# A hybrid decoder block on one core: Strassen lows in two pieces, a pause between two fetches into one stage, and a shorter list behind the output units

## The chip, the cores and the metric

The kernel runs on one core of a Trainium2 chip. The metric is the device time of one execution in microseconds (us). Before the change three runs took 2387.95, 2391.85 and 2394.31 us; the median, 2391.85, is the time before.

## The reference

For T = 256 tokens and D = 4096 channels, all in float32:

```python
h = rmsnorm(x, norm_w)
proj = einsum('bsd,de->bse', h, w_in)             # 4096 -> 20480 columns
u_p, z_p, u_c, b_c, c_c, z_c, g_logit = split(proj)
y_pool = causal_multiscale_pool(u_p, pool_w, pool_scale) * silu(z_p)
y_conv = causal_gated_shortconv(u_c, b_c, c_c, conv_w, conv_b) * silu(z_c)
br = einsum('bsnc,ncd->bsnd', stack([y_pool, y_conv]), w_branch)
merged = sum(sigmoid(g_logit + gate_b) * br, over the two branches)
x = x + einsum('bsd,de->bse', merged, w_out)
return rmsnorm(x, final_norm_w)
```

Three large products (`w_in`, `w_branch`, `w_out`) make up nearly all of the work; the mixers between them are short.

## The kernel before

**Numbers in two parts.** Every float32 operand is split into a *high* (a copy rounded to the matmul's format, by ScalarE, `act`, line 59) and a *low* (operand less high, by VectorE, `sub` through line 62). A product is three matmuls: high by high, low by high, high by low. TensorE is PE in the profile, VectorE DVE, ScalarE ACT, GpSimd POOL, SyncE SP.

**Units and steps.** A unit makes 1024 output columns (`NU`) for all tokens, in 16 steps of 256 rows of the contraction (8 in the branch units). The units run one after the other: those of `w_in` (the last two gate units are g1_3 and g1_0), then `w_branch` (b0_0, b1_0, ... b1_3), then `w_out` (o0 to o3). A step is plain (P) or a Strassen step (S), which needs seven products instead of eight on sums and differences of the four blocks of the weights; S steps use the banks `shared` beside `sums`.

**Weights.** A step's weights, four blocks of 128x512, are loaded by SP into one of five slots `raw` (some parts by POOL's queue, with accumulation). `ring` has 26 cells of 128x512 for highs and lows. For an S step ACT writes the highs of blocks 0 to 2 (one 128x1536 instruction where the cells lie side by side), DVE writes their lows (`whole`), and then DVE overwrites the slot: block 1 with block 3 less block 1 (`raw<-raw 128x512`), then blocks 0 and 2 with their differences from the new block 1 (128x1024). From these the four *formed* operands come, in two pairs, `outer` and `inner`, each a high of 128x1024 on ACT and a low of 128x1024 on DVE.

**Activations.** The left operands lie in `arena` (`last_pair` and `side` hold a few). While the last gate unit and the first branch unit run, the places of x's operands are refilled with y's (kept in DRAM as `y_d`), and later with those of the merged m (`m_d`). A `Fill` does that: a 256 KB fetch into one of three stages `sa`, `sb`, `sc` (issued on ACT's queue, line 83), after `LANDING` ticks the Strassen sums on DVE (S operands only), the high `arena<-sa` on ACT and the low `arena<-sa,arena` on DVE, which is the last reader of the stage.

**What sets the order.** Every instruction is pinned to program order on its engine. A *tick* is six matmuls. At each tick one item is popped from `queue`, the list of the work that follows a finished unit, and `pop_fill` takes one step of one `Fill` or issues one fetch. `gap(n)` is n empty items; `flush()` issues all that is left of the list at once. The list of an output unit (`epi` in `out_unit`) adds x's rows to the result `E` (POOL's accumulating transfers `E<-in_x_dram`, after those of the Strassen corners `E<-J`), loads the final norm's weights into `Y`, squares the two halves of `E` on ACT (`Y<-E`, with the sums of squares into `ossq`), multiplies `E` by the weights on DVE (`E<-E,Y`), and stores the result (`o_d`). The list of o0 is worked off while o1 runs, and so on; o3 has its own ending (`finish`), before which `flush()` and `last.before()`, the load of its final weights, are called at a fixed step.

Of the kernel before, what the change touches and what calls it, by code (L numbers as in the profile page):

```python
# [15 lines left out]
P = 128  # L16
# [3 lines left out]
NU = 1024  # L20
# [31 lines left out]
def hybrid_block(ctx: ExitStack, tc: tile.TileContext, x, xc, prm, rows_in, w_in, pool_w, w_branch, w_out, out):  # L52
# [11 lines left out]
    def mul(dst, a, b):  # L64
        return tt(dst, a, b, ALU.mult)
# [16 lines left out]
    def move(dst, src):  # L82
        return pin(nc.scalar.dma_start(dst, src))
# [140 lines left out]
    rg = Ring()  # L224

    def runs(cells):
        at = 0
        while at < len(cells):
            n = 1
            while at + n < len(cells) and cells[at + n] == cells[at] + n:  # L230
                n += 1
            yield slice(at, at + n), slice(cells[at], cells[at] + n)
            at += n

    def pieces(a, b):
        at = 0
        while at < len(a):
            n = 1
            while at + n < len(a) and a[at + n] == a[at] + n and b[at + n] == b[at] + n:
                n += 1  # L240
            yield slice(at, at + n), slice(a[at], a[at] + n), slice(b[at], b[at] + n)
            at += n

    def highs(cells, src):
# [3 lines left out]
    def lows(to, cells, src):  # L248
        for i, c, o in pieces(cells, to):
            sub(ring[:, o], src[:, i], ring[:, c].bitcast(F32))  # L250
# [7 lines left out]
    class Step:  # L258
# [28 lines left out]
        def rest(self):  # L287
            if self.kind == "P":
                def rests(to):
                    self.lows = to  # L290
                    if self in steps[:2]:
                        for i in range(4):
                            if self is steps[0] and i % 2 == 0:
                                x_low(0, 1 - i // 2)
                            lows(to[i:i + 1], self.cells[i:i + 1], self.q[:, i:i + 1])
                    elif self.halved:
                        for i in (0, 2):
                            lows(to[i:i + 2], self.cells[i:i + 2], self.q[:, i:i + 2])
                    else:
                        lows(to, self.cells, self.q)  # L300

                return [(4, None, rests)] + self.mid
            if self.kind == "S":
                def whole(to):
                    self.lows = to
                    lows(to, self.cells, self.q[:, 0:3])

                def outer(cells):
                    q = self.q
                    self.outer = cells  # L310
# [191 lines left out]
    def gap(n):  # L502
        return [None] * n
# [264 lines left out]
    def out_unit(c):  # L768
        cs = slice(c * NU, (c + 1) * NU)

        def start():
            move(Y[:, 0], final_w[None, cs].to_broadcast([P, NU]))

        def epi(u):
            def row(t):
                gather(E[:, t], xrows[:, t, cs])

            def square(t):
                act(Y[:, 1], E[:, t], AF.Square, accum_out=ossq[:, t, c:c + 1])
            return gap(6) + [lambda: row(0), None, lambda: row(1)] + gap(12) + [start] + gap(8) + [  # L780
                lambda: square(0), lambda: square(1),
                lambda: mul(E, E, Y[:, 0:1].to_broadcast([P, 2, NU]))] + gap(5) + [lambda: move(o_d[c], E)]

        text = (SIX5, NINE, NINE, OUT3)[c]
        u = Unit(f"o{c}", lambda i: w_out[c, i], seq_x(text), m_ops, epi, before=start if c == 3 else None)
        u.late = c < 3
        units.append(u)
# [16 lines left out]
    class Fill:  # L804
# [9 lines left out]
        def advance(self, force):  # L814
            o, q = self.o, self.st[:, 0:self.o.n] if self.o.kind == "S" else self.st[:, 4:8]
            if not force and (now[0] < self.due or (self.phase != 1 and now[0] < quiet[0])):
                return False
            if self.phase == 0 and o.kind == "S":
                sums_s(self.st)
                self.phase, self.due = 1, now[0] + 4  # L820
            elif self.phase < 2:
                act(o.view[:, 0], q)
                self.phase, self.due = 2, now[0] + 1
            else:
                sub(o.view[:, 1], q, o.view[:, 0].bitcast(F32))
                o.ready = True
                fills.remove(self)
            return True

    stages = [sa]  # L830
    fills = deque()
    now, quiet, hush = [0], [0], [0]
    LANDING, STORED, QUIET, HUSH = 12, 7, 5, 20

    def pop_fill(force=None):
        now[0] += 1
        for f in list(fills):
            if f.at is not None and f.free() and (now[0] >= f.at + LANDING or f.o is force):
                if f.advance(f.o is force):
                    break  # L840
        used = [f.st for f in fills if f.at is not None]
        nxt = next((f for f in fills if f.at is None), None)
        if nxt is None or not nxt.ready() or now[0] < hush[0]:
            return
        st = next((q for q in stages if not any(q is u for u in used)), None)
        if st is not None:
            nxt.fetch(st)

# [334 lines left out]
    for st in lead:  # L1183
# [1 line left out]
        run_step(last, st)  # L1185
        state["now"] += 1
        pump()
        if st is lead[len(lead) // 2]:
            flush()
            last.before()  # L1190
        if not combined and last.closed(FB):
# [83 lines left out]
```

## Time and profile before

| | |
|---|---|
| runs | 2387.95, 2391.85, 2394.31 us |
| profiled execution, its own time | 2388.57 us |
| its span (first to last instruction) | 2386.9 us |
| mean granted TensorE clock | 0.995 |
| ACT busy / DVE busy / POOL busy | 1489.8 / 2140.5 / 288.3 us |
| mean DMA rate | 263 GB/s |

How to read the rows: a row of the timeline gives start and length in us, engine, source line, operation, what is written from what is read, the number of instructions drawn together, and in brackets how long the engine had been idle before it and what released it. `ACTq` is ACT's sequencer issuing a transfer. In rows of groups stand the number, busy time, mean duration in ns, and the idle time before. The line is mostly that of a helper, so tiles tell instructions apart. The profiled execution's time is 1.7 us longer than its span.

### The profile page before, as it was taken

Reading aid. Unit: us, or ns where it says so; the run is one execution under the profiler, and the core shown is the slowest. Engines: PE = TensorE matmul, PEld = TensorE weight load, DVE = VectorE, ACT = ScalarE, POOL = GpSimd, SP = SyncE. Lnnn points to the kernel's source line nnn. Section 1 sums busy time; section 2 is a strip of 40 time slices with the busy share of each in tenths; the row PEclk is TensorE's granted clock in tenths of the full one; section 3 lists DMA queues with packets and bytes.
Section 4 is the critical chain, followed back from the end, with each engine's and each line's share of the span. In section 5 each row is a group of like instructions: output and inputs, shape, how many; then the busy total and the mean of one; then the engine's idle time right before and its main releaser. Section 6 shows DMA issues by size and latency. Waiting matters only on the chain. (4 is left out here: it accounts for less than half of the span.)

```text
span 2386.9 us, 28585 instructions
## 1 busy us (share of the span) xinstructions
PE 2349.5 (98%) x10424; PEld 1938.9 (81%) x10424; DVE 2140.5 (90%) x1986; ACT 1489.8 (62%) x1565; POOL 288.3 (12%) x342
## 2 busy tenths in 40 slices
PE   9999999999999999999999999999899999999997
PEld 7888888888888888888888888887778887878885
DVE  8799988999979979979999999987798889899997
ACT  6665655756656656656766676665656556566664
POOL 0001100111001201201111111110000000011110
PEclk9999999999999999999999999999999999999999
DMA  9789877988868768768999999999869788879996
GB/s 385 240 255 280 251 239 215 282 259 250 265 219 244 264 206 248 256 203 253 289 277 279 281 310 285 282 277 281 260 206 292 252 256 290 263 220 283 295 268 256
DMA packets 167709, 627.68 MB, mean 263 GB/s; under 512 B 17424, under 2 KB 25872, under 8 KB 135568
## 3 DMA queue, kind: packets, MB, share of 16 engines
q1 hardware_dynamic: 101792, 485.40, 56.6%
q0 software_dynamic: 48128, 98.59, 23.3%
q10 hardware_dynamic: 17648, 41.87, 4.9%
q8 instruction: 81, 1.33, 0.2%
q14 instruction: 60, 0.49, 0.1%
HBM read 579.66 MB, written 25.17 MB: 253 GB/s over the span
## 5 line engine op out<-in xcount | busy, mean ns | idle before, releaser
L59 ACT ACTIVATE ring<-raw 128x1024 fp32r<-128x1024 f32 (+3 forms) x1089 | 1226.6, 1172 | 768.9 <-DVE raw L62 530.1
L1053 PE MATMUL sums<-ring,arena 128*128 128x512 f32 x7011 | 1647.0, 390 | 20.5 <-DVE ring L62 10.1
L62 DVE TENSOR_TENSOR ring<-raw,ring 128x1024 fp32r<-128x1024 f32 (+3 forms) x1116 | 1452.0, 1338 | 135.2 <-ACT ring L59 66.9
L1053 PEld LDWEIGHTS sums<-ring,arena 128*128 128x128 f32 x7011 | 1314.5, 188 | 301.0 <-DVE ring L62 15.7
L1053 PE MATMUL shared<-ring,arena 128*128 128x512 f32 x2241 | 541.9, 389 | 0.8 <-DVE ring L62 0.8
L1053 PEld LDWEIGHTS shared<-ring,arena 128*128 128x128 f32 x2241 | 420.7, 188 | 89.1 <-DVE ring L62 1.5
L62 DVE TENSOR_TENSOR raw<-raw 128x512 f32<-128x512 f32 (+1 forms) x444 | 425.6, 959 | 16.6 <-DMA raw<-in_w_out_dram 2.4
L89 POOL DMA_DIRECT2D raw<-in_w_in_dram x168 | 145.5, 866 | 1361.3 <-DMA raw<-in_w_in_dram 688.3
L62 DVE TENSOR_TENSOR J<-J 128x512 f32<-128x512 f32 (+1 forms) x90 | 78.2, 869 | 16.2 <-ACT J L59 14.0
L1053 PE MATMUL sums<-ring,last_pair 128*128 128x512 f32 x306 | 78.1, 396 | 2.3 <-DVE ring L62 2.3
L59 ACT ACTIVATE J<-shared 128x512 f32<-128x512 f32 x128 | 69.7, 599 | 5.5 <-PE shared L483 2.0
L1053 PEld LDWEIGHTS sums<-ring,last_pair 128*128 128x128 f32 x306 | 58.5, 191 | 15.1 <-DVE ring L62 2.7
L59 ACT ACTIVATE E<-sums 128x512 f32<-128x512 f32 x76 | 42.1, 597 | 27.5 <-PE sums L1053 26.5
L89 POOL DMA_DIRECT2D raw<-in_w_out_dram x31 | 27.4, 883 | 262.4 <-DMA raw<-in_w_out_dram 99.7
L89 POOL DMA_DIRECT2D raw<-in_w_branch_dram x23 | 20.0, 869 | 314.2 <-DVE ring L62 127.5
L1053 PE MATMUL shared<-ring,last_pair 128*128 128x512 f32 x216 | 51.9, 389 | 0.0
L1053 PE MATMUL shared<-ring,side 128*128 128x512 f32 x207 | 50.7, 389 | 0.0
L1053 PEld LDWEIGHTS shared<-ring,last_pair 128*128 128x128 f32 x216 | 40.5, 188 | 8.4
L1053 PEld LDWEIGHTS shared<-ring,side 128*128 128x128 f32 x207 | 38.9, 188 | 8.1
L89 POOL DMA_DIRECT2D E<-J x28 | 38.9, 1469 | 17.3 <-ACT ring L59 17.3
L62 DVE TENSOR_TENSOR E<-E,Y 128x2048 f32<-128x2048 f32 x9 | 20.6, 2290 | 10.0 <-ACT Y L59 10.0
L59 ACT ACTIVATE E<-E 128x1024 f32<-128x1024 f32 x16 | 16.7, 1049 | 11.4 <-DMA E<-in_x_dram 11.4
(121 smaller groups left out, 596.7 us busy)
## 6 DMA issues: line engine op xcount, KB each, us to landing
raw<-in_w_in_dram SPq DMA_DIRECT2D x150, 1024.0 KB, 7.3
raw<-in_w_in_dram SPq DMA_DIRECT2D x168, 768.0 KB, 6.6
raw<-in_w_in_dram SPq DMA_DIRECT2D x176, 256.0 KB, 5.1
raw<-in_w_in_dram POOLq DMA_DIRECT2D x168, 256.0 KB, 6.7
raw<-in_w_branch_dram SPq DMA_DIRECT2D x41, 1024.0 KB, 7.0
raw<-in_w_out_dram SPq DMA_DIRECT2D x33, 1024.0 KB, 7.0
raw<-in_w_out_dram SPq DMA_DIRECT2D x31, 768.0 KB, 7.4
raw<-in_w_branch_dram SPq DMA_DIRECT2D x23, 768.0 KB, 6.1
```

The lines of the kernel that those rows point to most:

```text
L59: return pin(nc.scalar.activation(dst, src, func, **kw))
L62: return pin(nc.vector.tensor_tensor(out=dst, in0=a, in1=b, op=op))
L89: return pin(nc.gpsimd.dma_start(dst, src, accum_op=ALU.add))
L1053: pin(nc.tensor.matmul(ps, lhs, rhs, start=n == 0, stop=n == u.total[b] - 1))
```

## The change

1. `whole` makes the low of block 1 first, as one 128x512, and then those of blocks 0 and 2 as one instruction with a stride (128x2x512). For that `pieces` and `runs` may step by two. Where the cells wrap around the ring's end there are three of 128x512.
2. When a `Fill` has finished, its stage rests for five ticks (`REST`) before the next fetch may go into it. `LANDING` is 8 ticks instead of 12.
3. The list of an output unit is 28 items long instead of 39: three empty items instead of six before the first row, three instead of twelve before the load of `Y`, nine instead of eight before the first square, one between the squares, four instead of five before the store. In o3 the `flush()` and the load of `Y` come at the tenth of 13 steps instead of the seventh; by then the shorter list is empty.

```diff
     def pieces(a, b):
         at = 0
         while at < len(a):
-            n = 1
-            while at + n < len(a) and a[at + n] == a[at] + n and b[at + n] == b[at] + n:
+            n, d = 1, 1
+            if at + 1 < len(a) and a[at + 1] - a[at] == b[at + 1] - b[at] in (1, 2):
+                n, d = 2, a[at + 1] - a[at]
+            while n > 1 and at + n < len(a) and a[at + n] - a[at + n - 1] == b[at + n] - b[at + n - 1] == d:
                 n += 1
...
                 def whole(to):
                     self.lows = to
-                    lows(to, self.cells, self.q[:, 0:3])
+                    c, q = self.cells, self.q
+                    lows(to[1:2], c[1:2], q[:, 1:2])
+                    lows([to[0], to[2]], [c[0], c[2]], q[:, 0:3:2])
...
-            return gap(6) + [lambda: row(0), None, lambda: row(1)] + gap(12) + [start] + gap(8) + [
-                lambda: square(0), lambda: square(1),
-                lambda: mul(E, E, Y[:, 0:1].to_broadcast([P, 2, NU]))] + gap(5) + [lambda: move(o_d[c], E)]
+            return gap(3) + [lambda: row(0), None, lambda: row(1)] + gap(3) + [start] + gap(9) + [
+                lambda: square(0), None, lambda: square(1),
+                lambda: mul(E, E, Y[:, 0:1].to_broadcast([P, 2, NU]))] + gap(4) + [lambda: move(o_d[c], E)]
...
                 fills.remove(self)
+                rested[id(self.st)] = now[0] + REST
...
-    LANDING, STORED, QUIET, HUSH = 12, 7, 5, 20
+    LANDING, STORED, QUIET, HUSH, REST = 8, 7, 5, 20, 5
+    rested = {}
...
-        st = next((q for q in stages if not any(q is u for u in used)), None)
+        st = next((q for q in stages if not any(q is u for u in used) and now[0] >= rested.get(id(q), 0)), None)
...
-        if st is lead[len(lead) // 2]:
+        if st is lead[-4]:
             flush()
             last.before()
```

**First place: ACT in b0_0, where the y operands are fetched (about 1721 to 1733 us in the profile).** Before, the two fetches into `sb` and `sc` stand between the copies of the banks `shared` into `J`, ahead of the copies `E<-sums`:

```order
L59 ACTIVATE arena<-sb 128x1024
L59 ACTIVATE J<-shared_85 128x512
L83 DMA sb<-y_d 128x512
L59 ACTIVATE J<-shared_86 128x512
L59 ACTIVATE J<-shared_88 128x512
L83 DMA sc<-y_d 128x512
L59 ACTIVATE ring<-raw 128x1024 x2
L59 ACTIVATE J<-shared_87 128x512
L59 ACTIVATE ring<-raw 128x1536
L59 ACTIVATE E<-sums_82 128x512
L59 ACTIVATE E<-sums_84 128x512
```

The same place on ACT after the change:

```order
L59 ACTIVATE arena<-sb 128x1024
L59 ACTIVATE J<-shared_85 128x512
L59 ACTIVATE J<-shared_86 128x512
L59 ACTIVATE J<-shared_88 128x512
L59 ACTIVATE ring<-raw 128x1024 x2
L59 ACTIVATE J<-shared_87 128x512
L59 ACTIVATE ring<-raw 128x1536
L59 ACTIVATE E<-sums_82 128x512
L59 ACTIVATE E<-sums_84 128x512
L83 DMA sb<-y_d 128x512
L59 ACTIVATE E<-sums_81 128x512
L59 ACTIVATE E<-sums_83 128x512
```

The fetch into `sb` has moved behind two of the copies `E<-sums`; that into `sc` comes later still.

**Second place: ACT in o1, where the list of o0 is worked off (about 2157 to 2179 us).** Before, from the load of `Y` to the squares:

```order
L83 DMA Y<-in_rows_dram 128x1024
L59 ACTIVATE ring<-raw 128x1024 x4
L59 ACTIVATE ring<-raw 128x1536
L59 ACTIVATE ring<-raw 128x1024
L59 ACTIVATE side<-sa 128x512
L59 ACTIVATE ring<-raw 128x1024 x3
L59 ACTIVATE Y,ossq<-E 128x1024 x2
```

After:

```order
L83 DMA Y<-in_rows_dram 128x1024
L59 ACTIVATE ring<-raw 128x1024 x2
L59 ACTIVATE ring<-raw 128x1536
L83 DMA sa<-m_d 128x512
L59 ACTIVATE ring<-raw 128x1024 x2
L59 ACTIVATE ring<-raw 128x1536
L59 ACTIVATE Y,ossq<-E 128x1024 x2
L59 ACTIVATE ring<-raw 128x1024 x4
L59 ACTIVATE ring<-raw 128x1536
```

The squares have moved ahead of nine ring highs: the four of 128x1024 that before began at 2162.84 us, the next 128x1536, and four more. On DVE, at the same place, the product stood behind the lows of the following step:

```order
L62 TENSOR_TENSOR ring<-raw,ring 128x1024 x4
L62 TENSOR_TENSOR sa<-sa 128x128 x4
L62 TENSOR_TENSOR ring<-raw,ring 128x1536
L62 TENSOR_TENSOR raw<-raw 128x512
L62 TENSOR_TENSOR raw<-raw 128x2x512
L62 TENSOR_TENSOR ring<-raw,ring 128x1024 x2
L62 TENSOR_TENSOR side<-sa,side 128x512
L62 TENSOR_TENSOR E<-E,Y 128x2048
```

After the change it stands between the first of those four lows and the second:

```order
L62 TENSOR_TENSOR ring<-raw,ring 128x512
L62 TENSOR_TENSOR ring<-raw,ring 128x2x512
L62 TENSOR_TENSOR raw<-raw 128x512
L62 TENSOR_TENSOR raw<-raw 128x2x512
L62 TENSOR_TENSOR ring<-raw,ring 128x1024
L62 TENSOR_TENSOR E<-E,Y 128x2048
L62 TENSOR_TENSOR ring<-raw,ring 128x1024 x3
```

These rows also show the split low: two instructions, 128x512 and 128x2x512, where one of 128x1536 stood, ahead of the two that overwrite the slot.

**Third place: POOL in o3, where the list of o2 is worked off (about 2295 to 2335 us).** Before, a weight load stands between the two transfers of x's rows:

```order
L89 DMA E<-J 128x2x512
L89 DMA raw<-in_w_out_dram 128x512
L89 DMA E<-J 128x2x512
L89 DMA E<-in_x_dram 128x1024
L89 DMA raw<-in_w_out_dram 128x512
L89 DMA E<-in_x_dram 128x1024
L89 DMA raw<-in_w_out_dram 128x512 x2
```

After, both rows go ahead of it:

```order
L89 DMA E<-J 128x2x512
L89 DMA raw<-in_w_out_dram 128x512
L89 DMA E<-J 128x2x512
L89 DMA E<-in_x_dram 128x1024 x2
L89 DMA raw<-in_w_out_dram 128x512 x3
```

In the other output units POOL's order is unchanged.

More of the change, by code (lines that the diff above doesn't have):

```diff
@@ L226, in runs @@
     def runs(cells):
-        at = 0
-        while at < len(cells):
-            n = 1
[L230 to L233, printed above, removed]
+        for i, c, _ in pieces(cells, cells):
+            yield i, c
     def pieces(a, b):
@@ L237, in pieces @@
         while at < len(a):
-            n = 1
-            while at + n < len(a) and a[at + n] == a[at] + n and b[at + n] == b[at] + n:
+            n, d = 1, 1
+            if at + 1 < len(a) and a[at + 1] - a[at] == b[at + 1] - b[at] in (1, 2):
+                n, d = 2, a[at + 1] - a[at]
+            while n > 1 and at + n < len(a) and a[at + n] - a[at + n - 1] == b[at + n] - b[at + n - 1] == d:
                 n += 1
-            yield slice(at, at + n), slice(a[at], a[at] + n), slice(b[at], b[at] + n)
+            yield slice(at, at + n), slice(a[at], a[at] + d * (n - 1) + 1, d), slice(b[at], b[at] + d * (n - 1) + 1, d)
             at += n
```

## The prediction

> **What bounds the kernel now.** I read the page first, then the waits of TensorE, the busy time by stage, and, at each place where TensorE stands still, the timelines of the engines that feed it.
>
> ```profile
> PE 2349.5 (98%) x10424; PEld 1938.9 (81%) x10424; DVE 2140.5 (90%) x1986; ACT 1489.8 (62%) x1565; POOL 288.3 (12%) x342
> ...
> PE sums L1053 <- DVE ring L62: 12.3, 12, 2.3
> ```
>
> TensorE (PE) is busy for 2349.5 of 2386.9 us, and the change takes no matmul away. What it can win is the rest, 37.4 us; of its waits (us in all, times, longest) that for DVE's lows is the largest. By stage:
>
> ```profile
> 1640.00:1770.00 130.00, 118.72 (x501) 95.56 (x500) 108.23 (x116) 76.39 (x84) 7.76 (x9) 0.96 0.74 234
> ...
> 1945.00:2126.00 181.00, 174.54 (x769) 141.83 (x768) 160.22 (x158) 108.40 (x119) 14.27 (x16) 0.99 0.82 257
> 2126.00:2300.00 174.00, 174.00 (x770) 144.01 (x768) 161.28 (x143) 108.50 (x115) 26.23 (x28) 1.00 0.91 272
> ...
> 2300.00:2386.00 86.00, 71.51 (x313) 58.22 (x311) 68.83 (x74) 42.70 (x49) 6.53 (x7) 0.94 0.81 275
> ```
>
> The second number is the stretch, the third PE's busy time. While the y operands are fetched (1640 to 1770, units g1_0 to b1_0) PE is idle for 11.3 us, while the m operands are fetched (1945 to 2126) for 6.5 us, and in o1 and o2 (2126 to 2300) for none. These are the three terms of the sum: the first two can only fall, the third can only rise.
>
> **The later fetch, y operands.**
>
> ```profile
> 1668.45 2.14 PE L1053 MATMUL sums<-ring,last_pair 128*128 128x512 f32 x7 [2.27 <-DVE ring L62]
> ...
> 1731.39 8.90 PE L1053 MATMUL sums<-ring,arena 128*128 128x512 f32 x31 [6.09 <-ACT E L59]
> ...
> 1760.87 4.37 PE L1053 MATMUL sums<-ring,arena 128*128 128x512 f32 x18 [1.54 <-DVE ring L62]
> ```
>
> ```profile
> 1667.29 0.33 ACTq L83 DMA_DIRECT2D sc<-y_d  x1
> 1667.72 1.49 ACT L59 ACTIVATE ring<-raw 128x1536 fp32r<-128x1536 f32 x1 [1.18 <-DVE arena L62]
> ...
> 1726.99 2.00 ACT L59 ACTIVATE ring<-raw 128x1024 fp32r<-128x1024 f32 x2 [1.72 <-DVE arena L62]
> ...
> 1730.75 2.05 ACT L59 ACTIVATE E<-sums 128x512 f32<-128x512 f32 x4
> ```
>
> A fetch is issued by ACT, and it overwrites the stage that DVE's low (`arena`) still reads. ACT itself waits for that low (1.18 and 1.72 us in these rows), and behind the issue in ACT's order stand the highs for the next weights and, at 1730.75, the copies of the banks (`E<-sums`) for which PE waits 6.09 us. With five ticks of rest (a tick is six matmuls of 2349.5 / 10424 = 0.225 us, so 6.8 us) the low is done before ACT comes to the issue, and the issue costs its 0.33 us. The first order piece shows that both issues leave the place ahead of `E<-sums`. Stall by stall: 2.27 goes; 6.09 shrinks to about 2.3, because ACT comes to `E<-sums` earlier by 1.72 and by what the issue before it held (1.18 of the same kind), and 0.6 of issues, about 3.8 with what the earlier highs give; 1.54 falls to 0.6, since DVE runs less late. The rest of the 11.3, 1.4 in small stalls of the same kind, goes too: 2.27 + 3.8 + 0.9 + 1.4 = 8.4 us of idle time. The ends: 11.3 if every stall goes, 6 if 2.27 and 3.8 alone are won. I stand nearer the upper end, because every one of these waits lies behind a fetch that moves.
>
> Can the later fetch be late for its reader? It is given less time to land, 8 ticks instead of 12, or 10.8 us.
>
> ```profile
> DMA to landing us min/median/max: 3.2/6.6/9.2
> ```
>
> This is the landing of `sa` in the stretch: the longest is 9.2 us, 1.6 under 10.8. The fetch is 5 ticks later, its use allowed 4 earlier; the high comes out one tick later at worst. I cost it at nothing; the cover is that 1.6 us.
>
> **The later fetch, m operands.**
>
> ```profile
> 2013.78 6.89 PE L1053 MATMUL sums<-ring,arena 128*128 128x512 f32 x29 [1.66 <-DVE ring L62]
> ...
> 2025.34 25.24 PE L1053 MATMUL sums<-ring,arena 128*128 128x512 f32 x110 [1.05 <-DVE ring L62]
> ...
> 2119.43 0.73 PE L1053 MATMUL sums<-ring,arena 128*128 128x512 f32 x2 [2.33 <-ACT arena L59]
> ```
>
> ```profile
> 2118.44 0.93 ACT L59 ACTIVATE arena<-sa 128x896 fp32r<-128x896 f32 x1
> ```
>
> The last operand's high stands at 2118.44 behind four ring highs, and PE waits for it. With the shorter landing it stands behind two of the four, some 2 us earlier: 1.9 won. 0.9 of 1.66 and 1.0 of 1.05 follow as for y, and 0.9 of the 1.4 in small ones. Together 4.7 us, between 2.5 (half of the three rows) and 6.5 (the whole stage).
>
> **The shorter list of a w_out unit.** The list of o0 runs in o1, that of o1 in o2, that of o2 in o3. Its squares (ACT) need x's rows, added into `E` by POOL's accumulating transfers.
>
> ```profile
> 2154.96 0.86 POOL L89 DMA_DIRECT2D E<-in_x_dram  x1 [7.21 <-DMA E<-J]
> ...
> 2228.87 1.24 POOL L89 DMA_DIRECT2D E<-in_x_dram  x1
> 2239.66 0.86 POOL L89 DMA_DIRECT2D E<-in_x_dram  x1 [9.55 <-DMA E<-J]
> ...
> 2308.53 1.81 POOL L89 DMA_DIRECT2D E<-in_x_dram  x1
> ...
> 2321.16 0.86 POOL L89 DMA_DIRECT2D E<-in_x_dram  x1 [7.23 <-DMA E<-J]
> ...
> DMA to landing us min/median/max: 12.9/12.9/12.9
> ...
> DMA to landing us min/median/max: 11.6/14.6/17.7
> ...
> DMA to landing us min/median/max: 10.6/13.0/15.5
> ```
>
> POOL stands idle for `E<-J` before each second row, so three ticks fewer in the list bring it no earlier. The last three rows are landings: of the second row in o1, and of both rows in o2 and o3 (least the second, most the first). The second rows land at 2154.96 + 12.9 = 2167.8, 2239.66 + 11.6 = 2251.3 and 2321.16 + 10.6 = 2331.8. Now look at what surrounds the new places of the squares in o1 and o2:
>
> ```profile
> 2162.84 4.09 ACT L59 ACTIVATE ring<-raw 128x1024 fp32r<-128x1024 f32 x4 [2.69 <-PE sums L1053]
> ...
> 2163.94 4.66 DVE L62 TENSOR_TENSOR ring<-raw,ring 128x1024 fp32r<-128x1024 f32 x4
> ...
> 2168.70 2.88 PE L1053 MATMUL shared<-ring,arena 128*128 128x512 f32 x12
> ...
> 2249.68 2.88 PE L1053 MATMUL shared<-ring,arena 128*128 128x512 f32 x12
> ...
> L62 DVE TENSOR_TENSOR E<-E,Y 128x2048 f32<-128x2048 f32 x9 | 20.6, 2290 | 10.0 <-ACT Y L59 10.0
> ```
>
> In o1 both squares now stand ahead of these four highs. The second waits for 2167.8 and ends at 2169.1 (1.06 and the readout); the first high follows, its low ends near 2171.4. PE reads that low in the fifth matmul of the twelve that begin at 2168.70, at 2169.6: +1.9 us. Then the product `E<-E,Y` (2.29 us) stands between the first low and the second, which ends at 2174.8 where PE wants it at 2171.0 + 1.9: another +2.0, in all 3.9. In o2 the first square stands ahead of the third ring high and the second after it, so the second waits until 2251.3; by the same steps from the twelve that begin at 2249.68 the third low is 2.9 late, and the product pushes the next one to 4.8 in all. So the cover is gone in both: +8.7 us. Its ends: 0, if the highs and lows that already lie in the ring carry PE over; 8.7 plus each microsecond by which a row lands later.
>
> In o3 it is the other way.
>
> ```profile
> 2331.83 1.06 ACT L59 ACTIVATE Y<-E 128x1024 f32<-128x1024 f32 x1 [6.21 <-DMA E<-in_x_dram]
> ...
> 2337.03 1.43 PE L1053 MATMUL sums<-ring,arena 128*128 128x512 f32 x5 [1.96 <-DVE ring L62]
> ...
> 2340.16 2.12 PE L1053 MATMUL shared<-ring,arena 128*128 128x512 f32 x8 [0.76 <-DVE ring L62]
> ```
>
> Here the early `flush()` already puts the squares ahead of the row, and PE waits 1.96 and 0.76 behind them. The squares keep their place but for one ring high. But POOL now issues the second row ahead of a weight load that stood before it in the same queue (third order piece). In o2, with no load between them, the second row lands 4.7 us after the first (2251.3 less 2228.87 + 17.7); in o3 7.8 us after it (2331.8 less 2308.53 + 15.5). Taken as in o2, it lands 3 us earlier, and both waits go: −2.7; ends −2.7 and 0, if the row only takes as long as the 11.6 and 12.9 of the other units.
>
> **The split low of a Strassen step.**
>
> ```profile
> L62 DVE TENSOR_TENSOR ring<-raw,ring 128x1024 fp32r<-128x1024 f32 x834 | 989.5, 1223 | 68.6 <-PE sums L1053 39.5 <-ACT ring L59 25.9
> ...
> L62 DVE TENSOR_TENSOR ring<-raw,ring 128x1536 fp32r<-128x1536 f32 x184 | 323.0, 1755 | 40.9 <-ACT ring L59 19.6 <-PE sums L1053 7.8 <-ACT E L59 6.1
> ...
> L62 DVE TENSOR_TENSOR ring<-raw,ring 128x512 fp32r<-128x512 f32 x46 | 31.4, 687 | 4.4 <-ACT ring L59 4.1
> ...
> 2343.56 1.76 DVE ring L62
> 2345.34 0.70 DVE raw L62
> 2346.07 1.24 DVE raw L62
> ```
>
> No low with a stride stands in the trace; the strided difference of the same size, the last row, takes 1.24 us, and a plain low 1.22, so I take 1223 ns. Alone, 687 + 1223 ns replace 1755: +155 ns, 184 times, 28.5 us of DVE. But four lows of 1223 took 4.66 us above, a pitch of 1146 ns: an instruction that doesn't wait for its neighbour starts some 80 ns before that one's end. The difference `raw` after the low did wait (2345.34 less 2343.56 is 1.78, more than 1755). Afterwards it overwrites the middle block, whose low is two instructions back. So 607 + 1143 = 1750 against 1780: −30 ns a step at best, +125 if the new order helps nothing. That is −6 to +23 us of DVE, which has 246 idle; PE would see it only where it waits for a low, and takes it as 0, ends 0 and +1.9 (0.155 at each of the 12 waits). By the Trainium skill, "VectorE: DVE Perf Modes", section "The DRAIN you can't avoid", the next operation starts only when the pipe is empty and a semaphore costs nothing; by that the split would cost its 28.5 us of DVE whole. The trace's pitch of 1146 ns for lows of 1223 disagrees (the section itself excepts operations that aren't held).
>
> **The sum.** A wait that goes is worth some 0.16 us more than its row shows: a row counts the last matmul before it with its whole duration, and while the pitch is 0.23 us (twelve matmuls take 2.88 us, 110 take 25.24), twelve pitches are 2.72. For some twelve waits that go that is 1.9 us. So −8.4 − 4.7 − 2.7 − 1.9 + 8.7 + 0 = −9.0 us. The profiled run took 2388.57; it lies 3.3 under the median of 2391.85, which I take as the level that counts, so the predicted time is 2391.85 − 9.0, or 2383.
>
> **Rivals.**
> 1. The out units cost nothing, because ACT and DVE run far enough ahead in the ring: −17.7, 2374. For it: PE had no idle time there at all. Against: the lows in question end 4 to 5 us before their use (first low near 2165.2, used at 2169.6), and the squares' wait takes 6.2. 15%.
> 2. Half of the fetches' gain only, because the next stall moves up (`E<-sums` or a later arena high takes the place of the fetch): half of 14.7 (8.4 + 4.7, and 1.6 of the 1.9), so −7.3 + 8.7 − 3.0 = −1.6, 2390. For it: DVE is 90% busy, and part of the stalls are charged to `ring` lows. 25%.
> 3. Slower: the rows land later. The load of the final weights into `Y` now starts beside the second `E<-J`, and the squares stand so early that PE loses each microsecond of a later landing, three times. From 4.4 us per row on it decides (without o3's 3.0 the gains are 14.7, 7.2 more make it measurably slower: 14.7 + 7.2 − 8.7 = 13.2 over three units). At 6 us: 2391.85 − 14.7 + 8.7 + 18 = 2404. Landings above differ by 2.3 us, those of `sa` by 6. 10%.
> 4. The split doesn't spare the wait: +125 ns a step on DVE. At the waits +1.9, and as much again where it meets the out units' lateness: −9 + 4 = −5, 2387. 5%.
>
> **How the numbers follow.** A measurement here tells about 0.3%, 7.2 us, from no change: faster is below 2384.7. The forecast has 45%, with a range of its own of −14 to −4 (2378 to 2388), two thirds of it faster: 0.31, and with rival 1 0.46. Same: 0.12 of the forecast, rival 2 but 0.03, rival 4: 0.41. Slower: rival 3 and 0.03 for worse than rival 2: 0.13. The range of 8 in 10 takes in rival 1 with 3 us to spare and rival 2, and leaves out the worse half of rival 3: 2371 to 2396.
>
> **What would show it.** PE's idle time in the y stretch falls from 11.3 to about 2, in the m stretch from 6.5 to 1.5. ACT's `ring` rows after a fetch no longer name DVE `arena`. In o1 and o2 new PE waits for `ring` lows, of 2 to 3 us each, two per unit, with ACT `Y<-E` waiting for `E<-in_x_dram` before them; in o3 the wait of 6.21 is gone. Rows of DVE `raw` 128x512 start before the 128x2x512 low ends. The prediction fails if o1 and o2 stay without idle time, or if the fetch stretches keep theirs.

## The result, and the profile after

The changed kernel takes 2385.38 us (median of 16 runs, 2379.93 to 2389.32), the kernel before 2394.14 us in the same sessions (2387.95 to 2398.84). The ratio is 0.9966 with a 95% interval of 0.9957 to 0.9974: 8 us faster, where 9 were forecast. The profiled execution of the change took 2385.66 us, with a span of 2383.9 and a clock of 0.995.

The page and the waits of TensorE over the whole span of the changed kernel:

```profile
PE 2346.6 (98%) x10424; PEld 1938.5 (81%) x10424; DVE 2138.2 (90%) x2208; ACT 1488.3 (62%) x1565; POOL 287.0 (12%) x342
...
PE sums L1054 <- DVE ring L62: 11.1, 8, 3.0
PE shared L1054 <- ACT ring L59: 5.5, 2, 4.5
```

The wait for `ACT E` that was 6.6 us is no longer among the largest, and a new one stands there: 5.5 us for highs (`ring`) of ACT. By stage (the columns as before; the third from the end is TensorE's granted clock):

```profile
1640.00:1770.00 130.00, 126.54 (x555) 103.56 (x554) 118.34 (x130) 84.62 (x93) 9.49 (x11) 1.00 0.84 261
...
1945.00:2126.00 181.00, 177.70 (x798) 146.53 (x797) 167.57 (x184) 111.36 (x123) 14.66 (x16) 1.00 0.83 255
2126.00:2300.00 174.00, 165.19 (x714) 134.63 (x713) 151.10 (x151) 102.00 (x107) 24.94 (x28) 0.98 0.90 266
2300.00:2386.00 86.00, 66.78 (x287) 54.46 (x285) 61.89 (x73) 37.40 (x44) 5.83 (x7) 0.90 0.73 248
```

TensorE's idle time in the y stretch fell from 11.3 to 3.5 us, in the m stretch from 6.5 to 3.3, and where o1 and o2 run it rose from none to 8.8. What is left of the y stretch, and ACT at the place of the first order piece:

```profile
1719.36 3.03 PE L1054 MATMUL sums<-ring,arena 128*128 128x512 f32 x12 [1.09 <-ACT E L59]
...
1748.44 3.92 PE L1054 MATMUL sums<-ring,arena 128*128 128x512 f32 x16 [1.88 <-DVE ring L62]
```

```profile
1717.03 0.37 ACTq L83 DMA_DIRECT2D sb<-y_d  x1
1717.33 1.49 ACT L59 ACTIVATE ring<-raw 128x1536 fp32r<-128x1536 f32 x1
1718.71 2.06 ACT L59 ACTIVATE E<-sums 128x512 f32<-128x512 f32 x4
```

The fetch is issued while ACT works, with no bracket of idle time behind it, and `E<-sums` costs PE 1.09 us instead of 6.09. In o1 the order piece on the squares turned out as follows (POOL, then ACT, PE and DVE):

```profile
2142.54 0.86 POOL L89 DMA_DIRECT2D E<-in_x_dram  x1 [11.22 <-DMA E<-J]
...
2149.05 1.06 ACT L59 ACTIVATE Y<-E 128x1024 f32<-128x1024 f32 x1 [7.45 <-DMA E<-in_x_dram]
...
2153.36 1.06 ACT L59 ACTIVATE Y<-E 128x1024 f32<-128x1024 f32 x1 [3.17 <-DMA E<-in_x_dram]
...
2154.42 5.26 ACT L59 ACTIVATE ring<-raw 128x1024 fp32r<-128x1024 f32 x5
...
2155.51 0.79 PE L1054 MATMUL shared<-ring,arena 128*128 128x512 f32 x1 [4.46 <-ACT ring L59]
2156.77 2.93 PE L1054 MATMUL shared<-ring,arena 128*128 128x512 f32 x6 [0.47 <-DVE ring L62]
2160.10 1.14 PE L1054 MATMUL shared<-ring,arena 128*128 128x512 f32 x2 [0.41 <-DVE ring L62]
...
2155.49 1.22 DVE L62 TENSOR_TENSOR ring<-raw,ring 128x1024 fp32r<-128x1024 f32 x1 [7.75 <-ACT ring L59]
2156.63 2.29 DVE L62 TENSOR_TENSOR E<-E,Y 128x2048 f32<-128x2048 f32 x1
```

ACT stands 10.6 us for x's rows. PE waits 4.46 us for the first high behind the squares, 0.47 for that high's low, and 0.41 for the next low, which stands behind the product.

**A ledger.** Both kernels run the same 10424 matmuls in the same order, so the start of the n-th one can be compared between any two traces. Differences to the first profile of before, in us (minus is earlier); the ending is the time from the last matmul's start to the span's end:

| matmuls | what runs | forecast | change | change again | before again |
|---|---|---|---|---|---|
| to 7400 | w_in | 0 | −0.2 | 0.2 | 0.2 |
| 7400 to 7800 | y operands | −8.4 | −12.2 | −10.6 | 0.0 |
| 7800 to 8600 | branches | 0 | 0.5 | 0.1 | 0.5 |
| 8600 to 9400 | m operands | −4.7 | −6.6 | −6.6 | 0.9 |
| 9400 to 9600 | o1 | 3.9 | 8.2 | 8.7 | 0.0 |
| 9600 to 10000 | o2 | 4.8 | 4.3 | 7.7 | 0.0 |
| 10000 to the last | o3 | −2.7 | 0.6 | −1.0 | 2.5 |
| ending | | 0 | 2.4 | −0.3 | 2.9 |
| span | | | −3.0 | −1.7 | 7.0 |

(The forecast's 1.9 us for the uncounted part of the waits belongs to the y, m and o3 rows.) The last two columns are two of the experiments below.

**What the rows of the ledger are made of.** Only a part of each row is idle time of TensorE. Differences to the first profile of before, in us:

| stage | idle time: forecast | change | again | the rest of the row: change | again |
|---|---|---|---|---|---|
| y operands | −8.4 | −7.8 | −7.8 | −4.4 | −2.8 |
| m operands | −4.7 | −3.2 | −3.3 | −3.4 | −3.4 |
| o1 | 3.9 | 5.3 | 6.3 | 2.8 | 2.4 |
| o2 | 4.8 | 3.5 | 3.6 | 0.8 | 4.2 |
| o3 | −2.7 | −0.7 | −1.0 | 1.3 | 0.0 |

The rest lies in the matmuls around and behind a wait. The last one before it counts with its whole duration (the 0.16 us of the forecast), and the first one behind it is followed after 0.34 us instead of 0.23, which is 0.11 more. Behind some waits the granted clock also stood at 0.50, for 3.41 us or twice that. Each 3.41 us held some eight matmuls, 0.43 us apart, and so cost some 1.6 us. Before, this happened behind the waits of 2.27, 6.09 and 2.33 us; in the change it happened behind the 4.46 us in o1 and behind a wait of 2.06 us in o3. Four windows show it: one of before (behind 2.27), one of the change in o1, one of the change in o2, and one of its second profile in o2:

```profile
1669.95:1673.35 3.40, 3.40 (x9) 2.64 (x8) 3.33 (x4) 1.16 (x2) 0.00 (x0) 0.50 1.02 422
```

```profile
2154.20:2161.01 6.81, 4.62 (x9) 2.92 (x10) 5.52 (x4) 5.47 (x7) 0.62 (x1) 0.50 0.18 50
...
2241.00:2251.00 10.00, 6.53 (x27) 4.50 (x26) 8.46 (x8) 5.13 (x7) 0.86 (x1) 1.00 0.88 223
```

```profile
2248.00:2254.80 6.80, 6.08 (x15) 4.30 (x14) 6.76 (x7) 1.92 (x3) 0.78 (x1) 0.50 0.81 224
```

No length of a wait tells here whether the clock falls: a wait of 3.02 us in the change's m stretch went without it, and the wait of 1.9 us at matmul 7751 had it in the second profile of the change and not in the first.

### The profile page after: what moved, and what is told of

Read it like the earlier page. It is cut to its first block, busy times and chain, and to the rows that moved or that the text cites. A ratio compares the mean times of both kernels' runs of the same rounds, so it can differ in the third digit from the quotient of the medians.

```text
span 2383.9 us, 28821 instructions
## 1 busy us (share of the span) xinstructions
PE 2346.6 (98%) x10424; PEld 1938.5 (81%) x10424; DVE 2138.2 (90%) x2208; ACT 1488.3 (62%) x1565; POOL 287.0 (12%) x342
## 4 chain that ended last, share of the span: by engine, by line
PE 89%; DMA 4%; DVE 3%; issue 2%; ACT 1%; POOL 0%; SPq 0%; DVEq 0%; ACTq 0%; POOLq 0%
PE sums L1054 64%; PE shared L1054 23%; DVE ring L62 2%; DMA raw<-in_w_out_dram 1%; PE shared L696 1%; DMA E<-in_x_dram 1%; DMA raw<-in_w_branch_dram 1%; PE shared L482 1%; ACT ring L59 1%; DMA E<-J 1%; DMA raw<-in_w_in_dram 1%; DMA raw<-in_x_dram 0%; DVE E L62 0%; DVE raw L62 0%; POOL E L89 0%
## 5 line engine op out<-in xcount | busy, mean ns | idle before, releaser
L62 DVE TENSOR_TENSOR ring<-raw,ring 128x1024 fp32r<-128x1024 f32 (+2 forms) x1338 | 1467.2, 1141 | 147.8 <-ACT ring L59 73.8
L62 DVE TENSOR_TENSOR J<-J 128x512 f32<-128x512 f32 (+1 forms) x90 | 78.2, 869 | 14.7 <-ACT J L59 12.5
L1054 PEld LDWEIGHTS sums<-ring,last_pair 128*128 128x128 f32 x306 | 57.4, 188 | 11.9
```

Of the source, the lines that this page charges most:

```text
L62: return pin(nc.vector.tensor_tensor(out=dst, in0=a, in1=b, op=op))
L1054: pin(nc.tensor.matmul(ps, lhs, rhs, start=n == 0, stop=n == u.total[b] - 1))
```

## The experiments

Each kernel's ratio is that of its runs to those of the kernel before in the same session.

**The fetch rules alone.**

```diff
-    LANDING, STORED, QUIET, HUSH = 12, 7, 5, 20
+    LANDING, STORED, QUIET, HUSH, REST = 8, 7, 5, 20, 5
...
+                rested[id(self.st)] = now[0] + REST
```

> The kernel before with the fetch rules alone (rest of five ticks, landing of eight). My theory, that the fetches win what the traces show between 1640 and 2126 us (TensorE 12.2 us earlier in the y stretch and 6.5 more in the m stretch): 14 to 19 us faster than before, ratio 0.992 to 0.994, and no new waits in o1 and o2. The rival, that the output units' list costs nothing and the fetches win only the 8 us that the whole change won: ratio about 0.9965.

Measured: 2376.48 us, ratio 0.9926 (0.9908 to 0.9943), 17.7 us faster: twice the whole change. In the ledger −11.9 for y, −5.2 for m, +1.9 in o1, 0.1 in o2. The 1.9 us in o1 are a new wait of 1.6 us for a low, which I had not expected. The rival, that the fetches win only 8 us, falls.

**The list of the output units and the later flush alone.**

```diff
-            return gap(6) + [lambda: row(0), None, lambda: row(1)] + gap(12) + [start] + gap(8) + [
+            return gap(3) + [lambda: row(0), None, lambda: row(1)] + gap(3) + [start] + gap(9) + [
...
-        if st is lead[len(lead) // 2]:
+        if st is lead[-4]:
```

> The kernel before with the shorter list of the output units and the later flush alone. My theory: slower by 8 to 15 us, ratio 1.003 to 1.006, with TensorE idle in o1 (7 to 8 us) and o2 (about 4) behind squares that wait for x's rows, and a longer ending. The rival, that ACT and DVE run far enough ahead when the fetch rules are as before: ratio 1.000, no idle time in o1 and o2.

Measured: 2403.61 us, ratio 1.0038 (1.0026 to 1.0050), 9.1 us slower. The ledger has 5.0 in o1 and 7.4 in o2 (idle time 4.2 and 3.4), and −0.8 in o3. Another 4.3 us are lost among the branch units, where the list does nothing yet; they are one late transfer (see the fetches on another queue). Waits between 2126 and 2300 us, of PE and of ACT:

```profile
PE shared L1053 <- DVE ring L62: 3.7, 4, 1.7
PE shared L1053 <- ACT ring L59: 3.4, 2, 1.7
...
ACT Y L59 <- DMA E<-in_x_dram: 15.1, 3, 7.3
```

ACT waits 15.1 us for x's rows in three squares, and PE for what stands behind them. The third part of the change is a loss, with or without the fetch rules. (The longer ending did not appear here.)

**The split low alone.**

```diff
-                    lows(to, self.cells, self.q[:, 0:3])
+                    lows(to[1:2], c[1:2], q[:, 1:2])
+                    lows([to[0], to[2]], [c[0], c[2]], q[:, 0:3:2])
```

> The kernel before with the split low of a Strassen step alone. My theory: no change, ratio 0.999 to 1.001, VectorE's busy time within 10 us of before and its instructions two per step more. A rival: VectorE is late often enough that the earlier start of the difference wins 2 to 5 us (0.998 to 0.999). Another: two instructions for one cost TensorE 2 us or more (1.001 to 1.002).

Measured: 2391.67 us, ratio 0.9986 (0.9974 to 0.9999). In its ledger no row is over 0.7 us, and the last matmul starts 0.3 us later than before; VectorE's busy time is 2138.2 us against 2140.5, with 222 instructions more, little over one for each Strassen step and not two. So the runs hint at some 3 us that the trace doesn't show, and the next run doesn't bear it out.

**The fetch rules and the split, with the old list.** The change without its third part.

```diff
-            return gap(3) + [lambda: row(0), None, lambda: row(1)] + gap(3) + [start] + gap(9) + [
+            return gap(6) + [lambda: row(0), None, lambda: row(1)] + gap(12) + [start] + gap(8) + [
...
-        if st is lead[-4]:
+        if st is lead[len(lead) // 2]:
```

> The fetch rules and the split low, with the old list of the output units: the change without its third part. My theory: the same as the fetch rules alone, 14 to 19 us faster than before (0.992 to 0.994), so that the third part of the change gives back about half of the gain. The rival, that the list is free: no faster than the whole change, about 0.9965.

Measured: 2378.21 us, ratio 0.9932 (0.9918 to 0.9947), no better than the fetch rules alone (0.9926). o1 and o2 lose 1.3 and 0.0 us. From here to the whole change (0.9966) it is about 8 us: that is what the new list gives back.

**The whole change with later squares.**

```diff
-            return gap(3) + [lambda: row(0), None, lambda: row(1)] + gap(3) + [start] + gap(9) + [
+            return gap(3) + [lambda: row(0), None, lambda: row(1)] + gap(3) + [start] + gap(17) + [
```

> The whole change, but 17 empty items instead of nine before the first square, so that squares, product and store come eight ticks later (about 11 us); rows and the load of the final weights stay early. My theory, that the list costs because the squares stand on ACT before x's rows are in: TensorE's idle time in o1 and o2 (7.2 and 4.1 us) goes, and the kernel is as fast as without the third part, ratio to before 0.992 to 0.994. The rival, that the early rows and the early load of the weights cost it (contention of the transfers): it stays near the whole change, 0.996 to 0.997.

Measured: 2377.91 us, ratio 0.9930 (0.9911 to 0.9949). With squares, product and store eight ticks later, the loss in o1 falls from 8.2 to 1.6 us; in o2 3.9 stay (4.3 and 7.7 before). PE's waits between 2126 and 2300 us are now one row, and ACT's wait for x's rows is gone from that stretch:

```profile
PE sums L1054 <- DVE ring L62: 3.3, 2, 1.9
```

The 3.9 us in o2 are lost at another place than before: at matmul 9951, not between 9894 and 9911, PE waits 1.93 us for a low behind the product, and 3.41 us of half clock follow. Shown by the runs: most of the list's cost comes from the place of the squares and the product, since the early rows and the early load stay in this kernel. In the trace this holds for o1; in o2 the late product still costs a wait.

**The rest alone, landing still 12 ticks.**

```diff
-    LANDING, STORED, QUIET, HUSH = 12, 7, 5, 20
+    LANDING, STORED, QUIET, HUSH, REST = 12, 7, 5, 20, 5
```

> The kernel before with the rest of five ticks alone, landing still 12. My theory, that the gain comes from ACT no longer waiting at the issue of a fetch: most of the y stretch is won (10 to 12 us), of the m stretch some 3; ratio 0.994 to 0.996. If the shorter landing carries the gain instead: 0.999 or above, or slower, since five ticks are lost for each fetch.

Measured: 2408.34 us, ratio 1.0064 (1.0040 to 1.0087): 15 us slower, against my theory. At 1716 us of before its stream is 6.2 us ahead, as with both rules, and at 1743 us 14.8, more than the change's 13.6: ACT's waits at the issues are gone. Then the operands are late, and by the end of the y row 8.1 us are lost; the m row loses another 10.3. PE's waits between 1728 and 1785 us:

```profile
PE sums L1055 <- ACT arena L59: 8.3, 4, 2.7
PE sums L1055 <- DVE arena L62: 7.2, 4, 3.5
```

Three stages are refilled in a cycle: a fetch, its landing, sums, high and low, and now the rest. By these waits for `arena`, five ticks more per cycle are more than the units leave.

**The landing of eight ticks alone, no rest.**

```diff
-    LANDING, STORED, QUIET, HUSH = 12, 7, 5, 20
+    LANDING, STORED, QUIET, HUSH = 8, 7, 5, 20
```

> The kernel before with the landing of eight ticks alone, no rest. My theory: the high and low come four ticks earlier, but the next fetch still follows the low by a tick, so ACT waits at the issue as before; the y stretch wins little, the m stretch up to 3 us: ratio 0.998 to 1.001. If the landing carries the gain: 0.993 to 0.995.

Measured: 2388.66 us, ratio 0.9981 (0.9967 to 0.9995), some 4 us faster. The ledger: 7.2 us lost before matmul 7400, 5.6 and 5.3 won in the y and m rows, 4.3 and 1.6 lost in o1 and o2, though the list is the old one. ACT still waits at the issue, and PE for `E<-sums`, only elsewhere:

```profile
1660.11 0.33 ACTq L83 DMA_DIRECT2D sc<-y_d  x1
1660.48 1.49 ACT L59 ACTIVATE ring<-raw 128x1536 fp32r<-128x1536 f32 x1 [1.13 <-DVE arena L62]
...
1661.27 8.49 PE L1053 MATMUL sums<-ring,arena 128*128 128x512 f32 x29 [3.24 <-DVE ring L62]
...
1687.27 3.35 PE L1053 MATMUL sums<-ring,arena 128*128 128x512 f32 x7 [3.37 <-ACT E L59]
```

One rule loses 15 us, the other wins 4, both together win 18: the four ticks of landing pay for the five of rest.

**The kernels profiled again.** The kernel before, and the change, without an edit.

> The kernel before, profiled a second time, to see how far one execution's stages can be trusted. The profiled execution lies 5 to 6 us under the median of its runs. If that is luck of one stage, this profile shows the y and m stretches idle as before (11.3 and 6.5 us within 1 us) and its further microseconds in one place, such as a wait for a weight load; if it is drift spread over the whole span, every stretch is longer.

> The changed kernel, profiled a second time. Expected of its stages: the y and m stretches, o1 and o2 as in the first profile within 1 us each (8.2 and 4.3 us lost in o1 and o2), and the ending different by some us, as it was between the two profiles of the kernel before. If instead o1 or o2 differ by more than 2 us, their cost is luck of the transfers and not of the order.

Measured: before 2395.59 us (span 2393.9), change 2386.93 us (span 2385.2). The stages up to o2 repeat within 1 us in the kernel before; o3 is 2.5 us longer and the ending 2.9. The second profile of the change repeats its stages within 2 us (the y row, 1.6 apart, not within the 1 that I had expected) but for o2, which lost 7.7 us where it had lost 4.3. By the bound that I had set that would be luck of the transfers. The traces show luck of the clock: TensorE is idle in o2 for 3.5 us in the first and 3.6 us in the second, and nearly the whole difference lies in 6.83 us of half clock around the waits, which the first does not have. The same 29 matmuls, in the first and in the second:

```profile
2247.12 6.91 PE L1054 MATMUL sums<-ring,arena 128*128 128x512 f32 x29 [1.68 <-DVE ring L62]
```

```profile
2250.93 8.65 PE L1054 MATMUL sums<-ring,arena 128*128 128x512 f32 x29 [0.72 <-DVE ring L62]
```

The list alone lost 7.4 us in o2 with such a stretch, the last kernel below 4.7 without one. In the kernels with the old list o2 lost under 0.2, but 1.6 with the landing alone, where a half clock that began in o1 reaches into it. The ending hangs on one transfer, the last rows of x. Its row in the chain, in the first and second profile of before, then in the first and second of the change:

```profile
2356.60 8.90 DMA raw<-in_x_dram
```

```profile
2360.74 11.76 DMA raw<-in_x_dram
```

```profile
2351.21 11.37 DMA raw<-in_x_dram
```

```profile
2355.15 8.70 DMA raw<-in_x_dram
```

It takes 8.7 to 11.8 us in either kernel. Over the fourteen profiles of all kernels here it took 8.7 to 9.3 us in nine, and the ending is within 0.4 us of the first profile of before; in five it took 10.6 to 12.1 us, and the ending is 1.7 to 3.2 us longer. So the 2.4 us that the change's ending seemed to lose are not the change's. The second profile of before has 2.9 of its further us there and 2.5 in o3, where a wait of 3.88 us with half clock behind it stands in place of waits of 1.96 and 0.76.

**The fetches on another queue.** The kernel before, with the old rules; only the fetches leave ACT.

```diff
-            move(st[:, 4:8].rearrange("p o c -> p (o c)"), self.src)
+            aside(st[:, 4:8].rearrange("p o c -> p (o c)"), self.src)
```

> The kernel before, but its operand fetches (y and m) are issued on POOL's queue instead of ACT's, with the old landing and no rest. ACT then waits for no fetch. My theory, that the stalls come from ACT standing at the issue: PE's waits at 1668, 1731 and 1760 us shrink as with the fetch rules, 5 to 10 us in the y stretch, ratio 0.995 to 0.998, unless POOL's own loads, now queued behind the waiting fetches, come late. The rival, that the fetch rules win by the other order of highs and lows and not by ACT's waits: ratio 0.999 to 1.001, stalls as before.

Measured: 2376.89 us, ratio 0.9939 (0.9919 to 0.9959), some 15 us faster. The y row of the ledger is −13.8, the m row −5.0; 5.1 us are lost between them. They are one wait of 3.13 us at matmul 8154, with half clock behind it: VectorE's product there waits 7.47 us for an accumulating transfer `E<-J`, issued at matmul 8048 in every kernel, that took 23.9 us to land. It took 23.1 in the list alone and 22.3 in the fetch rules with the split, which lost 4.3 and 1.9 us there, and 20.4 to 21.4 in the other eleven profiles. Whether POOL's loads lengthened it here stays open; they need not have. PE's waits from 1640 to 1770 us, which before were 6.3 us for `ACT E` and 4.9 for `DVE ring`:

```profile
PE sums L1053 <- DVE ring L62: 2.4, 2, 1.9
```

With POOL at the issue the same stalls go without any rest. That ACT's standing at the issue caused them is shown, more strongly than I had expected.

**A rest of two ticks.** The fetch rules alone, with a shorter rest.

```diff
-    LANDING, STORED, QUIET, HUSH, REST = 8, 7, 5, 20, 5
+    LANDING, STORED, QUIET, HUSH, REST = 8, 7, 5, 20, 2
```

> The kernel before with landing eight and a rest of two ticks instead of five, nothing else. ACT waited 1.2 to 2.4 us at the issues, one to two ticks. My theory, that the rest only has to outlast DVE's low: two ticks win as much as five, ratio 0.992 to 0.994. The rival, that five ticks are needed because DVE lags by more than the waits show: 0.995 to 0.998, between landing alone (0.998) and both (0.993).

Measured: 2379.89 us, ratio 0.9943 (0.9925 to 0.9960), between my theory and the rival, and its interval overlaps that of five ticks. In the ledger the y row is −9.1 (−11.9 with five), the m row −6.9. What is missing is at `E<-sums`:

```profile
PE sums L1055 <- ACT E L59: 4.4, 3, 2.6
```

Behind the longest of these three waits follow 3.41 us of half clock. Two ticks outlast most lows, but fetches still stand ahead of some copies of the banks. Whether the 0.17% between the two rests are real can't be told from these runs.

**The load of the final weights later.** The whole change, squares and rows in place.

```diff
-            return gap(3) + [lambda: row(0), None, lambda: row(1)] + gap(3) + [start] + gap(9) + [
+            return gap(3) + [lambda: row(0), None, lambda: row(1)] + gap(10) + [start] + gap(2) + [
```

> The whole change, but the load of the final weights into Y goes seven ticks later (ten empty items before it and two after it); squares, product, rows and store keep their ticks, and VectorE's and POOL's order is the same. My theory on why o1 and o2 cost more than forecast: the early load of Y (512 KB) shares the transfers with the second E<-J, which took 13.3 to 16.3 us to land in the changed kernel and 10.1 to 13.1 with the old list. Then E<-J lands in 10 to 13 us again, x's second row comes some 3 us earlier, TensorE's loss in o1 falls from 8 to about 5 us and in o2 by 2 to 3, and the ratio to before falls from 0.9966 to 0.994 to 0.9955. The rival, that the rows are late because the weight loads lag behind a stream that runs faster: E<-J and the ratio stay as in the whole change, and product waits for Y may make it worse (0.9965 to 0.999).

Measured: 2383.04 us, ratio 0.9959 (0.9944 to 0.9973): the interval overlaps that of the whole change, so the time decides nothing. The landing does. The second `E<-J` of o0's list took, in the whole change, here, and with the old list (fetch rules and split):

```profile
DMA to landing us min/median/max: 14.2/14.2/14.2
```

```profile
DMA to landing us min/median/max: 11.8/11.8/11.8
```

```profile
DMA to landing us min/median/max: 10.8/10.8/10.8
```

In o2 and o3 it was 13.3 and 16.3 in the whole change, and 12.1 and 12.3 here. So the early load of `Y` does slow it by 1 to 4 us. The rival holds in part, though. POOL issues the second `E<-J` of o0's list when 9419 matmuls have begun before, 9435 in the whole change, 9434 here, and also 9434 with the old list (fetch rules alone, and with the split): so it goes out 15 matmuls, 3.4 us, later in the stream without the early load too. And in o1 the row's own transfer, which now has the load beside it, took 12.4 us instead of 10.7, and o1's loss fell only from 8.2 to 6.8; o2's, 4.7, is no less than 4.3. In o3, where it landed early enough, the ledger has −2.4: close to the −2.7 that I had forecast for the change itself.

## Why the prediction was right, point by point

- **The sum, −9.0 against −8.** Right, by terms that were each off by some us and cancelled; that it came so close is in part luck. The places were right, and but for o3 the waits. The step that was mis-sized in the y, m, o1 and o3 terms alike is the price of a wait: the prediction counts its row and 0.16 us. The traces show 0.27 us beyond the row, and half clock behind some waits. That was left out where waits go and where they come, and so it cancelled in good part. The prediction's own rows have it: a clock of 0.96 in the y stretch, and 31 matmuls in 8.90 us behind the 6.09 where twelve take 2.88, a pace at which 31 would take 7.2. That the sum has to be set against the median and not against the profiled run was right, and mattered: spans of the first two profiles differ by 3.0 us, the runs by 8.
- **y operands, −8.4 forecast, −12.2 and −10.6 measured.** The mechanism was right: ACT stood at the issue (the kernel with POOL's queue shows it). In idle time it came out near, 7.8 us of 11.3 against 8.4: 2.27 went, 6.09 shrank to 1.09 and not only to 2.3, but 1.54 grew to 1.88 where 0.6 was forecast, and a new one of 0.49 stands beside it. The further 4.4 us (2.8 in the second profile) are matmuls around the waits, 3.3 of them the half clock behind 2.27 and 6.09.
- **A later fetch costs nothing.** It held for both rules together, with 1.6 us of cover; the rest alone showed how thin it is: without the shorter landing operands come late and 15 us are lost.
- **m operands, −4.7 forecast, −6.6 measured.** In idle time it is 3.2 us, less than forecast: all of the 2.33 at the last operand went, not 1.9 of it, but the wait of 1.05 at 2025.34 us did not go and grew to 3.02. Of the other 3.4 us, 1.7 are the half clock behind the 2.33; the rest is the 0.27 at each wait that went.
- **o1 and o2, +8.7 forecast, 12.5 and 16.4 measured in the change, 12.4 with the list alone.** The place was right, and so was the order of the waits: squares for rows, highs behind squares, lows behind the product. The idle time is 5.3 + 3.5 us (6.3 + 3.6 in the second profile, 4.2 + 3.4 with the list alone): 8.8 against 8.7, but 1.4 more in o1 and 1.3 less in o2. What goes beyond is the price of these waits, half clock above all. "The rows land at 2154.96 + 12.9" was off in o1 as well. The second row was issued there when 9500 matmuls had begun, against 9473 before: 27 matmuls, 6 us later in the stream. 16 of them lie in the issue of the second `E<-J` (9435 against 9419; 9434 with the fetch rules and the old list, 9421 with the list alone), the others in its landing, 14.2 us against 11.7, beside the load of `Y`. I took the landings of before, and named only the second cause, as rival 3's mechanism; it came at 1 to 4 us, under the 4.4 from which it would have decided. In o2 the second row was issued at matmul 9847 against 9846, as forecast.
- **o3, −2.7 forecast, 0.6 and −1.0 measured.** `E<-J` needed 16.3 us there instead of 13.0, beside the load of `Y`, so that the second row was no earlier relative to the stream. In the first profile the second wait went, but the first stayed, 2.06 us for 1.96, and half clock behind it added 1.6; in the second profile waits of 1.07 and 0.68 stayed. With the load later, the gain was there (−2.4).
- **The split low, 0.** In the changed kernel the pair of lows and the two differences behind it read:

```profile
2163.17 1.82 DVE L62 TENSOR_TENSOR ring<-raw,ring 128x512 fp32r<-128x512 f32 x2
2164.91 1.94 DVE L62 TENSOR_TENSOR raw<-raw 128x512 f32<-128x512 f32 x2
```

  The difference starts 1.74 us after the first low (1.78 before), 0.08 before the second low's end: it no longer waits for its neighbour, and the step is 40 ns shorter instead of 155 longer. (The first of these rows draws 128x512 and 128x2x512 together.) VectorE's busy time is 2138.2 us, 2.3 less; no effect on TensorE is settled. By the Trainium skill, "VectorE: DVE Perf Modes", section "The DRAIN you can't avoid", a next operation that is not held starts earlier; the 0.08 us agree with that, and not with the section's first rule, by which it waits until the pipe is empty.
- **Rivals.** The first (squares cost nothing) fell with the list alone, 1.0038; the second (half of the fetches' gain) with the fetch rules alone, 0.9926; the fourth with the rows above.

A version beats both kernels: the fetch rules with the old list, 0.9926, 0.4% under the whole change.

## What to carry to other kernels

An issue that waits for a reader holds everything behind it on its engine: look for the rows of an engine that name a reader of the buffer as the releaser, and either issue from an idle engine's queue or delay the issue until the reader is surely done. When a delay is added in a cycle of few buffers, take the same time out of the cycle elsewhere, since each of the two rules alone was worth far less than both. When a list is shortened, ask of every item what it waits for: an item that stands earlier than its data stops its engine, and a transfer that is moved can lengthen the transfers beside which it lands. When a wait is priced, look at the matmuls behind it and at the granted clock there, and not only at its row.

## What the runs showed of the hardware

Behind some of TensorE's waits (2.27, 6.09 and 2.33 us before; 4.46 and 2.06 us in the change) its granted clock stood at 0.50 for 3.41 or 6.83 us, and matmuls began 0.43 us apart instead of 0.23. Not every such wait had it (3.02 us in the change did not), and nearly the same waits had it in one execution and not in another (o2 of the change, some 3 us of difference).

One transfer of 1 MB at the end, at the same place of the program, took 8.7 to 11.8 us from one execution to the next of the same kernel, and that alone moved the span by up to 3 us; a difference between two single profiles is no measure at this size. A 512 KB load issued 0.5 to 4.4 us behind an accumulating transfer went with a landing of that transfer of 13.3 to 16.3 us (second `E<-J`, twelve lists of the four profiles with the load that early), against 10.0 to 13.6 in the thirty lists of the other ten, where the load came 10 us or more behind it.
